# Token norms split in two steps, their squares summed on VectorE, in a hybrid decoder block

## The chip, the core and the metric

The kernel runs on one core of one Trainium2 chip. The metric is device time in microseconds of one execution of the whole program. Engines are named as the profile names them: PE is TensorE (matmuls), PEld its weight loads, DVE is VectorE, ACT is ScalarE, POOL is GpSimd, SP is SyncE, which issues most transfers. SBUF is the core's working memory of 128 partitions, PSUM the eight accumulator banks that TensorE writes.

## The reference

One decoder layer over 1024 tokens of 1024 channels, in float32: an RMS norm, one wide input projection that feeds a sparse attention and a pooling mixer, a gated merge with an output projection and a residual, then a second RMS norm, a squared-ReLU MLP with a residual, and a final RMS norm. What matters here are the last two norms and what stands around them:

```python
def rms_norm(x, g):
    xf = x.astype(jnp.float32)
    y = xf * lax.rsqrt(jnp.mean(xf * xf, axis=-1, keepdims=True) + EPS)
    return (y * g.astype(jnp.float32)).astype(x.dtype)
...
    x = x + (ga * a + gb * b) @ w_out
    h = rms_norm(x, norm_mlp)
    return x + jnp.square(jax.nn.relu(h @ w_ff1)) @ w_ff2
...
    return rms_norm(x, norm_final)
```

## The kernel before

The residual x lies transposed in SBUF: `acc` (printed as accx) holds eight blocks of 128 channels, each 1024 tokens wide, worked in two halves of 512 tokens. Because channels lie across partitions, the sum of squares of a token crosses partitions and is made by TensorE.

Every float32 matmul of 128x512 is done as three passes (L77 to L79, helper `mm3`): operands are split into a high part, cast by ACT (`whi`, `mv`, `mh`), and a low part, subtracted by VectorE (L82, `wlo`, `ml`). Weight tiles come through rings of a few buffers, so casts and subtractions work a few tiles ahead of TensorE.

A norm has these steps. Squares: `square_into` (L751) squares a finished block on ACT, the first into the sum `sqa`, each later one into `sq`, of which there is one buffer, and POOL adds it to `sqa` (L762); the last block's square stays apart. Sums: `sumsq_r` (L764) multiplies `sqa` and `sq` by a column of ones, one token block of 128 at a time, eight matmuls of one column (L769). Root: `rsqrt` (L117) is a chain of six small VectorE instructions (`rs_ms` to `rs_c`) with one square root on ACT between. Broadcast: `bcast` (L130) scales the identity by the four columns of roots into a tile that shares the buffer `sq` (L135), TensorE multiplies it by ones (L136), and ACT copies the result out of PSUM into `rB` (L137). Scaling: eight VectorE instructions multiply the blocks by gain and `rB`, into `h` (`normalise`, L785) or in place (`emit`, L880).

There are four such norms. The two ahead of the MLP are called norm 1 (first half of the tokens) and norm 2 (second half), the two final ones norm 3 and norm 4. Norm 1 stands between the second half's merge of branches (L798 to L812) and its output projection (L818 to L824). Norm 2 stands in the first MLP product, behind its step (1, 3) (L933). The MLP's two products are done by a scheme of seven half-size products with summed weights (PRODUCTS); in the second, each product p has eight steps j of 12 matmuls. Norm 3 is issued behind product 4 of the last round, whose results finish the first half, and norm 4 after product 3, the last (L971 to L973).

The framework orders the instructions of each engine from the order of the code and its own estimates; each engine runs its list in order and waits on semaphores.

Of the kernel before, what the change touches and what calls it, by code (L numbers as in the profile page):

```python
# [49 lines left out]
def build(tc, a, out, dbg=None):  # L50
# [697 lines left out]
    acc = accp.tile([P, NK, S], F32, name="accx")  # L748
    r2B = rB

    def square_into(sqs, src, m, sqa):  # L751
        n = src.shape[1]
        if m == 0:
            nc.scalar.activation(sqa[:, :n], src, AF.Square)
            sqs.append(sqa[:, :n])
        else:
            sq = accp.tile([P, HALF], F32, name="sq", bufs=1)[:, :n]
            nc.scalar.activation(sq, src, AF.Square)  # L758
            if m == NK - 1:
                sqs.append(sq)  # L760
            else:
                nc.gpsimd.tensor_tensor(sqa[:, :n], sqa[:, :n], sq, op=ADD)  # L762

    def sumsq_r(sqs, wk, ps_, dst):  # L764
        n = sqs[0].shape[1] // P
        ps = ps_()
        for j in range(n):
            for e, sq in enumerate(sqs):
                nc.tensor.matmul(ps[:, 2 * j:2 * j + 1], lhsT=sq[:, j * P:(j + 1) * P], rhs=ones[:, 0:1],  # L769
                                 start=e == 0, stop=e == len(sqs) - 1)  # L770
        col = wk.tile([P, NT], F32, name="rs_c", bufs=2)[:, :n]
        rsqrt(col, ps[:, 0:2 * n:2], wk, n)
        bcast(dst, col, ps_(), wk)

    psM = pool(root, "psM", bufs=8, space=PSUM)

    def bank():
        return psM.tile([P, HALF], F32, name="psm")
# [9 lines left out]
    with ExitStack() as st:  # L788
        wm = pool(st, "wm")
        for hf in range(2):  # L790
# [7 lines left out]
            for m in range(NK):  # L798
# [11 lines left out]
                nc.scalar.copy(mh, ta)  # L810
                sub(nc.vector, ml, ta, mh)
                mg.append((mh, ml))  # L812
            if hf == 1:
                sumsq_r(sqs, wm, bank, r2B[:, :HALF])
                normalise(0)
            sqa = accp.tile([P, HALF], F32, name="sqa", bufs=2)
            sqs = []
            for m in range(NK):  # L818
                wh, wl = load(cols(a["w_out"], m * P, P), nc.vector)
                nc.sync.dma_start(acc[:, m, sl], a["xT"][m * P:(m + 1) * P, sl])  # L820
                ps = bank()
                mm3(ps, [(wh[:, k], wl[:, k], mg[k][0], mg[k][1]) for k in range(NK)])
                nc.vector.scalar_tensor_tensor(acc[:, m, sl], ps, 0.5, acc[:, m, sl], op0=MUL, op1=ADD)
                square_into(sqs, acc[:, m, sl], m, sqa)  # L824
        dump("x2", acc)
    octx.close()

# [1 line left out]
    with ExitStack() as st:  # L829
# [43 lines left out]
            nc.scalar.activation(c, c, AF.Relu)  # L873
            nc.scalar.activation(c, c, AF.Square)

        def emit(n, sqs):
            sl = halves[n]
            sumsq_r(sqs, accp, bank, r2B[:, sl])
            for m in range(NK):
                nc.vector.scalar_tensor_tensor(acc[:, m, sl], acc[:, m, sl], gfin[:, m:m + 1], r2B[:, sl],  # L880
                                               op0=MUL, op1=MUL)
                if m % 2:
                    nc.sync.dma_start(out[(m - 1) * P:(m + 1) * P, sl].rearrange("(k p) t -> p k t", p=P),
                                      acc[:, m - 1:m + 1, sl])

        F = [wf.tile([P, S], F32, name=f"f{j}") for j in range(NF)]
        tt = nc.vector.tensor_tensor
        for fh in range(2):
# [4 lines left out]
            for pair in ((1, 2), (6,), (7, 4), (5, 3)):  # L893
# [9 lines left out]
                for p, j in steps:  # L903
# [26 lines left out]
                    elif p == 3:  # L930
                        tt(u, u, ps, op=ADD)
                        relu2(u)
                    if fh == 0 and (p, j) == (1, 3):  # L933
                        sumsq_r(sqs, accp, bank, r2B[:, HALF:])
                        normalise(1)


            if fh == 1:
                sqa_of = [accp.tile([P, HALF], F32, name="sqa", bufs=2) for _ in range(2)]
                fin = [[], []]  # L940
                nfin = [0, 0]

            def done(m, n):
                if fh == 1:
                    square_into(fin[n], acc[:, m, halves[n]], nfin[n], sqa_of[n])
                    nfin[n] += 1

            banks = {}
            group = {1: "x", 6: "x", 2: "y", 7: "z", 4: "z", 5: "w", 3: "w"}
            for p in (1, 2, 6, 7, 5, 4, 3):  # L950
                xt = PRODUCTS[p][1]
                fresh = group[p] not in banks
                if fresh:
                    banks[group[p]] = [bank() for _ in range(4)]
                ps = banks[group[p]]
                for j in range(JH):
                    xh, xl = moving([(blk_(k, n, j), sg_) for k, n, sg_ in xt])
                    wh, wl = weights("w_ff2", p, j)
                    for m in range(4):
                        mm3(ps[m], [(wh[:, m * P:(m + 1) * P], wl[:, m * P:(m + 1) * P], xh, xl)],  # L960
                            fresh and j == 0, j == JH - 1, not fresh)

                targets = {1: ((0, 0, 1),), 2: ((0, 0, 1),), 6: ((1, 1, -1), (1, 0, -1), (0, 1, 1)),
                           7: ((1, 1, 1),), 5: ((1, 1, -1),), 4: ((1, 0, 1),), 3: ((0, 1, 1),)}
                for m, n, sg_ in targets[p]:
                    for mi in range(4):
                        c = acc[:, m * 4 + mi, halves[n]]
                        tt(c, c, ps[mi], op=ADD if sg_ > 0 else SUB)
                        if p in (2, 5, 4, 3):
                            done(m * 4 + mi, n)  # L970
                if fh == 1 and p == 4:  # L971
                    emit(0, fin[0])
        emit(1, fin[1])  # L973
    root.close()


# [56 lines left out]
```

## Time and profile before

| | |
|---|---|
| median of 3 runs | 1509.44 us (1508.98 to 1510.2) |
| profiled execution, its own time | 1510.39 us |
| its span, first to last instruction | 1508.6 us |
| PE busy | 1451.2 us, 96% |
| DVE busy | 1001.3 us, 66% |
| ACT busy | 760.6 us, 50% |
| POOL busy | 187.6 us, 12% |
| mean granted clock of PE | 0.981 |

Busy shares are means over stages with different limits; a stage is read from the timeline around it. Matmul ends are modelled, so the pitch from start to start tells more than the durations. A float32 matmul of one column shows as two instructions. An engine's idle time is written behind the instruction that ended it, with what released it. The granted clock is a share of full speed: 1.00 is 2.4 GHz and 0.50 is 1.2 GHz.

### The profile page before, as it was taken

The page shows a single profiled execution, that of the slowest core. Times are in us where ns is not written, and L with a number is a line of the kernel's source. Part 1 is how long each engine was busy: PE and PEld are TensorE (multiplying, and loading weights), DVE is VectorE, ACT ScalarE, POOL GpSimd, SP SyncE. Part 2 cuts the span into 40 slices and gives each one's busy share as a digit, 9 for nine tenths or more (in the row PEclk, how much of TensorE's full clock was granted, in tenths as well). Part 3 has the DMA queues.
Part 4 walks back from the last instruction along what each step waited for, and adds up shares of the span by engine and source line. Part 5 has one row for each costly group of instructions (what it writes and reads, how often), then busy time and mean ns, then how long its engine had stood idle before and what let it go on. Part 6 is the DMA issues. An engine that isn't in the chain of part 4 may idle for free.

```text
span 1508.6 us, 20793 instructions
## 1 busy us (share of the span) xinstructions
PE 1451.2 (96%) x7369; PEld 1199.6 (80%) x7369; DVE 1001.3 (66%) x1928; ACT 760.6 (50%) x1561; POOL 187.6 (12%) x238
## 2 busy tenths in 40 slices
PE   8999999997999999999899999999999999999995
PEld 6788888886788878787687888888888888888874
DVE  5693451115888888777648368667897386679974
ACT  4454231115877877765334353674344545754441
POOL 2006323330111111110010100000000000001021
PEclk9999999998999999999999999999999999999997
DMA  8234217875668777867944333333332223332312
GB/s 304 70 99 148 70 49 192 213 191 147 179 162 201 177 184 178 196 157 188 323 136 147 113 91 98 96 93 97 98 98 92 97 86 103 98 98 84 109 53 112
DMA packets 130201, 204.67 MB, mean 136 GB/s; under 512 B 9904, under 2 KB 62896, under 8 KB 129584
## 3 DMA queue, kind: packets, MB, share of 16 engines
q1 hardware_dynamic: 112032, 136.22, 28.8%
q0 software_dynamic: 17920, 67.11, 19.5%
q8 instruction: 58, 0.95, 0.3%
q14 instruction: 47, 0.39, 0.1%
q10 hardware_dynamic: 144, 0.00, 0.0%
HBM read 186.52 MB, written 83.89 MB: 179 GB/s over the span
## 4 chain that ended last, share of the span: by engine, by line
PE 84%; DVE 6%; DMA 5%; ACT 3%; issue 1%; POOL 1%; SPq 0%; POOLq 0%; DVEq 0%; ACTq 0%
PE psm L78 16%; PE psm L77 16%; PE psm L79 16%; PE oacc L663 5%; PE psF L78 5%; PE psF L79 5%; PE psF L77 5%; PE psT L652 4%; PE psS L557 3%; PE psS L558 2%; PE psG L77 2%; PE psG L78 2%; PE psG L79 2%; DMA xt<-in_x 1%; PE psS L560 1%
## 5 line engine op out<-in xcount | busy, mean ns | idle before, releaser
L78 PE MATMUL psm<-mv,whi 128*128 128x512 f32 x896 | 351.5, 392 | 0.0
L79 PE MATMUL psm<-mv,wlo 128*128 128x512 f32 x896 | 351.3, 392 | 0.0
L77 PE MATMUL psm<-mv,whi 128*128 128x512 f32 x896 | 351.2, 392 | 0.0
L82 DVE TENSOR_TENSOR wlo<-wraw,whi 128x512 fp32r<-128x512 f32 x288 | 198.8, 694 | 98.8 <-ACT whi L866 70.2
L866 ACT CAST whi<-wraw 128x512 fp32r<-128x512 f32 x224 | 138.8, 620 | 247.8 <-PE psm L78 185.5
L78 PEld LDWEIGHTS psm<-mv,whi 128*128 128x128 f32 x896 | 168.7, 188 | 37.0
L77 PEld LDWEIGHTS psm<-mv,whi 128*128 128x128 f32 x896 | 168.7, 188 | 36.9
L79 PEld LDWEIGHTS psm<-mv,wlo 128*128 128x128 f32 x896 | 168.7, 188 | 36.6
L179 ACT CAST whi<-wraw 128x512 fp32r<-128x512 f32 x112 | 69.7, 622 | 124.5 <-PE psF L78 58.0
L762 POOL TENSOR_TENSOR sqa<-sqa,sq 128x512 f32<-128x512 f32 x24 | 33.4, 1392 | 734.3 <-ACT sq L758 734.3
L656 DVE TENSOR_TENSOR pl<-psT,ph 128x512 fp32r<-128x512 f32 (+1 forms) x160 | 102.0, 647 | 30.3 <-ACT ph L655 29.0
L655 ACT CAST ph<-psT 128x512 fp32r<-128x512 f32 (+1 forms) x160 | 87.8, 556 | 49.0 <-PE psT L652 47.2
L567 DVE TENSOR_REDUCE nm<-psS 128x1 f32<-128x64 f32 (+8 forms) x192 | 100.0, 540 | 17.2 <-PE psS L560 10.1
L82 POOL TENSOR_TENSOR wlo<-wraw,whi 128x512 fp32r<-128x512 f32 x48 | 65.6, 1368 | 108.1 <-ACT whi L179 88.2
L78 PE MATMUL psF<-xl,whi 128*128 128x512 f32 x192 | 74.7, 389 | 0.0
L77 PE MATMUL psF<-xh,whi 128*128 128x512 f32 x192 | 74.7, 389 | 0.0
L79 PE MATMUL psF<-xh,wlo 128*128 128x512 f32 x192 | 74.7, 389 | 0.0
L568 ACT ACTIVATE pS<-psS,nm 128x64 f32<-128x64 f32 (+8 forms) x128 | 68.0, 533 | 8.8 <-DVE nm L567 8.3
L846 ACT CAST mv<-mt 128x512 fp32r<-128x512 f32 x96 | 59.1, 617 | 20.0 <-DVE mt L844 15.5
L82 DVE TENSOR_TENSOR mv<-mt,mv 128x512 fp32r<-128x512 f32 x96 | 67.3, 708 | 1.1 <-ACT mv L846 0.6
L663 PE MATMUL oacc<-ph,vst 128*128 128x256 f32 x264 | 64.1, 318 | 1.2 <-ACT ph L655 0.9
L652 PE MATMUL psT<-cf,pS 128*128 128x128 f32 x352 | 60.4, 276 | 2.8 <-DVE pS L624 2.6
(242 smaller groups left out, 3034.7 us busy)
## 6 DMA issues: line engine op xcount, KB each, us to landing
wraw<-wsw_ff SPq DMA_DIRECT2D x128, 256.0 KB
wraw<-in_w_ff SPq DMA_DIRECT2D x96, 256.0 KB
wsw_ff<-in_w_ff POOLq DMA_DIRECT2D x16, 1024.0 KB, 9.4
wsw_ff<-wsw_ff POOLq DMA_DIRECT2D x16, 1024.0 KB, 9.3
wraw<-in_w_in SPq DMA_DIRECT2D x40, 256.0 KB
wraw<-in_w_out SPq DMA_DIRECT2D x32, 256.0 KB
xt<-in_x SPq DMA_DIRECT2D x8, 512.0 KB
qd<-q SPq DMA_DIRECT2D x16, 256.0 KB
```

The lines of the kernel that those rows point to most:

```text
L77: nc.tensor.matmul(ps, lhsT=sh, rhs=mh, start=first and i == 0, stop=False, skip_group_check=more)
L78: nc.tensor.matmul(ps, lhsT=sh, rhs=ml, start=False, stop=False, skip_group_check=more)
L79: nc.tensor.matmul(ps, lhsT=sl, rhs=mh, start=False, stop=last and i == n - 1, skip_group_check=more)
L82: eng.tensor_tensor(lo, src, f(hi), op=SUB)
L179: nc.scalar.copy(h, v)
L567: nc.vector.tensor_reduce(nm, v, axis=AX.X if flat else AX.XY, op=MAX, negate=True)
L568: nc.scalar.activation(p if flat else p.rearrange("p (a n) -> p a n", a=2), v, AF.Exp, bias=nm, accum_out=sm)
L652: nc.tensor.transpose(ps[:, j, e], src[e][:, c0:c0 + P], ident)
L655: nc.scalar.copy(ph[:, :n], ps[:, :n])
L656: nc.vector.tensor_tensor(pl[:, :n], ps[:, :n], f(ph[:, :n]), op=SUB)
L663: nc.tensor.matmul(o, lhsT=v, rhs=part[:rows, j], start=gi == 0 and j == 0 and part is ph, stop=2 * gi + j == nb - 1 and part is pl)
L866: nc.scalar.copy(hi, raw)
```

## The change

Four things change. The sums of squares are added on VectorE and not on POOL. `sumsq_r` is split: `stats` makes the sums and the root, and the broadcast is issued later, with matmuls of the running stage in between (norms 1 to 3). In the last product (p = 3) each of the four squares goes into a buffer of its own, taken from the ring of `mv`, and straight into the sums, so norm 4 has five tiles to sum and norm 3 one. `emit` multiplies by the broadcast where it lies in PSUM, without the copy into `rB`, and stores the last two blocks singly.

```diff
@@ -748,29 +748,28 @@
     acc = accp.tile([P, NK, S], F32, name="accx")
     r2B = rB
 
-    def square_into(sqs, src, m, sqa):
-        n = src.shape[1]
-        if m == 0:
-            nc.scalar.activation(sqa[:, :n], src, AF.Square)
-            sqs.append(sqa[:, :n])
+    def square_into(sqs, src, direct, sqa, sq=None):
+        if not sqs:
+            nc.scalar.activation(sqa, src, AF.Square)
+            sqs.append(sqa)
         else:
-            sq = accp.tile([P, HALF], F32, name="sq", bufs=1)[:, :n]
+            if sq is None:
+                sq = accp.tile([P, HALF], F32, name="sq", bufs=1)
             nc.scalar.activation(sq, src, AF.Square)
-            if m == NK - 1:
+            if direct:
                 sqs.append(sq)
             else:
-                nc.gpsimd.tensor_tensor(sqa[:, :n], sqa[:, :n], sq, op=ADD)
-
-    def sumsq_r(sqs, wk, ps_, dst):
-        n = sqs[0].shape[1] // P
-        ps = ps_()
-        for j in range(n):
-            for e, sq in enumerate(sqs):
+                nc.vector.tensor_tensor(sqa, sqa, sq, op=ADD)
+
+    def stats(sqs, wk):
+        ps = bank()
+        for e, sq in enumerate(sqs):
+            for j in range(4):
                 nc.tensor.matmul(ps[:, 2 * j:2 * j + 1], lhsT=sq[:, j * P:(j + 1) * P], rhs=ones[:, 0:1],
-                                 start=e == 0, stop=e == len(sqs) - 1)
-        col = wk.tile([P, NT], F32, name="rs_c", bufs=2)[:, :n]
-        rsqrt(col, ps[:, 0:2 * n:2], wk, n)
-        bcast(dst, col, ps_(), wk)
+                                 start=e == 0 and j == 0, stop=e == len(sqs) - 1 and j == 3)
+        col = wk.tile([P, NT], F32, name="rs_c", bufs=2)[:, :4]
+        rsqrt(col, ps[:, 0:8:2], wk, 4)
+        return col
 
     psM = pool(root, "psM", bufs=8, space=PSUM)
 
@@ -810,9 +809,7 @@
                 nc.scalar.copy(mh, ta)
                 sub(nc.vector, ml, ta, mh)
                 mg.append((mh, ml))
-            if hf == 1:
-                sumsq_r(sqs, wm, bank, r2B[:, :HALF])
-                normalise(0)
+            col = stats(sqs, wm) if hf == 1 else None
             sqa = accp.tile([P, HALF], F32, name="sqa", bufs=2)
             sqs = []
             for m in range(NK):
@@ -821,7 +818,10 @@
                 ps = bank()
                 mm3(ps, [(wh[:, k], wl[:, k], mg[k][0], mg[k][1]) for k in range(NK)])
                 nc.vector.scalar_tensor_tensor(acc[:, m, sl], ps, 0.5, acc[:, m, sl], op0=MUL, op1=ADD)
-                square_into(sqs, acc[:, m, sl], m, sqa)
+                square_into(sqs, acc[:, m, sl], m == NK - 1, sqa)
+                if hf == 1 and m == 0:
+                    bcast(r2B[:, :HALF], col, bank(), wm)
+                    normalise(0)
         dump("x2", acc)
     octx.close()
 
@@ -873,15 +873,20 @@
             nc.scalar.activation(c, c, AF.Relu)
             nc.scalar.activation(c, c, AF.Square)
 
-        def emit(n, sqs):
+        def emit(n, col):
             sl = halves[n]
-            sumsq_r(sqs, accp, bank, r2B[:, sl])
+            ps = bank()
+            dg = accp.tile([P, HALF], F32, name="sq", bufs=1)
+            for j in range(4):
+                js = slice(j * P, (j + 1) * P)
+                nc.vector.tensor_scalar(dg[:, js], ident, col[:, j:j + 1], None, op0=MUL)
+                nc.tensor.matmul(ps[:, js], lhsT=ones, rhs=dg[:, js], start=True, stop=True)
             for m in range(NK):
-                nc.vector.scalar_tensor_tensor(acc[:, m, sl], acc[:, m, sl], gfin[:, m:m + 1], r2B[:, sl],
-                                               op0=MUL, op1=MUL)
-                if m % 2:
-                    nc.sync.dma_start(out[(m - 1) * P:(m + 1) * P, sl].rearrange("(k p) t -> p k t", p=P),
-                                      acc[:, m - 1:m + 1, sl])
+                nc.vector.scalar_tensor_tensor(acc[:, m, sl], acc[:, m, sl], gfin[:, m:m + 1], ps, op0=MUL, op1=MUL)
+                step = 2 if m < NK - 2 else 1
+                if m % 2 or step == 1:
+                    nc.sync.dma_start(out[(m + 1 - step) * P:(m + 1) * P, sl].rearrange("(k p) t -> p k t", p=P),
+                                      acc[:, m + 1 - step:m + 1, sl])
 
         F = [wf.tile([P, S], F32, name=f"f{j}") for j in range(NF)]
         tt = nc.vector.tensor_tensor
@@ -930,20 +935,24 @@
                     elif p == 3:
                         tt(u, u, ps, op=ADD)
                         relu2(u)
-                    if fh == 0 and (p, j) == (1, 3):
-                        sumsq_r(sqs, accp, bank, r2B[:, HALF:])
+                    if fh == 0 and (p, j) == (1, 2):
+                        col = stats(sqs, accp)
+                    if fh == 0 and (p, j) == (1, 4):
+                        bcast(r2B[:, HALF:], col, bank(), accp)
                         normalise(1)
 
 
             if fh == 1:
                 sqa_of = [accp.tile([P, HALF], F32, name="sqa", bufs=2) for _ in range(2)]
                 fin = [[], []]
-                nfin = [0, 0]
 
             def done(m, n):
                 if fh == 1:
-                    square_into(fin[n], acc[:, m, halves[n]], nfin[n], sqa_of[n])
-                    nfin[n] += 1
+                    sq = None
+                    if p == 3:
+                        sq = xgp.tile([P, 2, HALF], F32, tag=f"xl{moving.n % MB}", name="sqd")[:, 0]
+                        moving.n += 1
+                    square_into(fin[n], acc[:, m, halves[n]], p == 3, sqa_of[n], sq)
 
             banks = {}
             group = {1: "x", 6: "x", 2: "y", 7: "z", 4: "z", 5: "w", 3: "w"}
@@ -959,6 +968,10 @@
                     for m in range(4):
                         mm3(ps[m], [(wh[:, m * P:(m + 1) * P], wl[:, m * P:(m + 1) * P], xh, xl)],
                             fresh and j == 0, j == JH - 1, not fresh)
+                    if fh == 1 and (p, j) == (3, 1):
+                        col = stats(fin[0], accp)
+                    if fh == 1 and (p, j) == (3, 2):
+                        emit(0, col)
 
                 targets = {1: ((0, 0, 1),), 2: ((0, 0, 1),), 6: ((1, 1, -1), (1, 0, -1), (0, 1, 1)),
                            7: ((1, 1, 1),), 5: ((1, 1, -1),), 4: ((1, 0, 1),), 3: ((0, 1, 1),)}
@@ -968,9 +981,7 @@
                         tt(c, c, ps[mi], op=ADD if sg_ > 0 else SUB)
                         if p in (2, 5, 4, 3):
                             done(m * 4 + mi, n)
-                if fh == 1 and p == 4:
-                    emit(0, fin[0])
-        emit(1, fin[1])
+        emit(1, stats(fin[1], accp))
     root.close()
 
 
```

VectorE at norm 1: before, the root (`rs_c`) is followed by the diagonal (`sq`) and all eight scalings into `h`, ahead of the next splits.

```order
L128 TENSOR_TENSOR rs_c<-rs_y,rs_t 128x4
L135 TENSOR_SCALAR sq<-cf,rs_c 128x128 x4
L785 SCALAR_TENSOR_TENSOR h_7964<-accx,cf,rB 128x512
L785 SCALAR_TENSOR_TENSOR h_7965<-accx,cf,rB 128x512
L785 SCALAR_TENSOR_TENSOR h_7966<-accx,cf,rB 128x512
L785 SCALAR_TENSOR_TENSOR h_7967<-accx,cf,rB 128x512
L785 SCALAR_TENSOR_TENSOR h_7968<-accx,cf,rB 128x512
L785 SCALAR_TENSOR_TENSOR h_7969<-accx,cf,rB 128x512
L785 SCALAR_TENSOR_TENSOR h_7970<-accx,cf,rB 128x512
L785 SCALAR_TENSOR_TENSOR h_7971<-accx,cf,rB 128x512
L82 TENSOR_TENSOR wlo<-wraw,whi 128x512
L823 SCALAR_TENSOR_TENSOR accx<-psm,accx 128x512
```

After, two splits of weight tiles and a residual add stand ahead of the scalings.

```order
L128 TENSOR_TENSOR rs_c<-rs_y,rs_t 128x4
L82 TENSOR_TENSOR wlo<-wraw,whi 128x512
L135 TENSOR_SCALAR sq<-cf,rs_c 128x128 x4
L820 SCALAR_TENSOR_TENSOR accx<-psm,accx 128x512
L82 TENSOR_TENSOR wlo<-wraw,whi 128x512
L784 SCALAR_TENSOR_TENSOR h_7964<-accx,cf,rB 128x512
L784 SCALAR_TENSOR_TENSOR h_7965<-accx,cf,rB 128x512
L784 SCALAR_TENSOR_TENSOR h_7966<-accx,cf,rB 128x512
```

The scalings (`h`) moved from ahead of the first residual add (`accx`) to behind it; six more of the eight follow the last row shown, then the second residual add and two splits.

PE at norm 3, in product 3 of the last round (`mv` are its moving operands, one tile for each step j): before, the first sum of ones and `sqa` stands behind one step, the rest in the next.

```order
L77 MATMUL psm<-mv_14325,whi 128x512
L78 MATMUL psm<-mv_14325,whi 128x512
L79 MATMUL psm<-mv_14325,wlo 128x512
L769 MATMUL psm<-ones,sqa 128x1
L77 MATMUL psm<-mv_14346,whi 128x512
L78 MATMUL psm<-mv_14346,whi 128x512
L79 MATMUL psm<-mv_14346,wlo 128x512
L77 MATMUL psm<-mv_14346,whi 128x512
L78 MATMUL psm<-mv_14346,whi 128x512
L769 MATMUL psm<-ones,sq 128x1
L769 MATMUL psm<-ones,sqa 128x1
```

After, four sums of `sqa` alone stand behind two steps and the first three matmuls of the third (`mv_14341`), and the broadcast behind that third step.

```order
L79 MATMUL psm<-mv_14341,wlo_14347 128x512
L768 MATMUL psm<-ones,sqa 128x1 x4
L77 MATMUL psm<-mv_14341,whi_14346 128x512
L78 MATMUL psm<-mv_14341,whi_14346 128x512
L79 MATMUL psm<-mv_14341,wlo_14347 128x512
L77 MATMUL psm<-mv_14341,whi_14346 128x512
L78 MATMUL psm<-mv_14341,whi_14346 128x512
L79 MATMUL psm<-mv_14341,wlo_14347 128x512
L77 MATMUL psm<-mv_14341,whi_14346 128x512
L78 MATMUL psm<-mv_14341,whi_14346 128x512
L79 MATMUL psm<-mv_14341,wlo_14347 128x512
L883 MATMUL psm<-sq,ones 128x128 x4
```

The sums moved from 12 matmuls behind product 4 to 27 behind it; between them and the broadcast (the line L883) stand nine matmuls.

VectorE at the same place after the change: the adds of squares stand between the residual adds, the splits of weights (`wlo`) and of moving operands (`mv`).

```order
L82 TENSOR_TENSOR mv_14427<-f_9185,mv_14427 128x512
L82 TENSOR_TENSOR wlo_14347<-wraw,whi_14346 128x512
L981 TENSOR_TENSOR accx<-accx,psm 128x512 x3
L762 TENSOR_TENSOR sqa<-sqa,sq 128x512
L981 TENSOR_TENSOR accx<-accx,psm 128x512
L82 TENSOR_TENSOR wlo<-wraw,whi 128x512
L762 TENSOR_TENSOR sqa<-sqa,sq 128x512
L82 TENSOR_TENSOR mv_14448<-f_9186,mv_14448 128x512
L82 TENSOR_TENSOR wlo<-wraw_14409,whi 128x512
L762 TENSOR_TENSOR sqa<-sqa,sq 128x512
L82 TENSOR_TENSOR mv_14469<-f_9187,mv_14469 128x512
L762 TENSOR_TENSOR sqa<-sqa,sq 128x512
```

Each add waits for its square on ACT; before, this list had the same splits without the adds.

## Rows read from the trace of the kernel before

**Rows 1.** Waits of PE, 760 to 1500 us: waiter, releaser, us in total, times, longest.

```profile
PE psm L769 <- POOL sqa L762: 7.6, 2, 4.8
PE psm L136 <- DVE sq L135: 5.0, 2, 3.1
```

**Rows 2.** Timeline of PE at norm 3: start, us, instruction, [idle before, releaser].

```profile
1454.73 0.39 PE L79 MATMUL psm<-mv,wlo 128*128 128x512 f32 x1
...
1457.45 0.39 PE L79 MATMUL psm<-mv,wlo 128*128 128x512 f32 x1
...
1460.61 0.38 PE L769 MATMUL psm<-ones,sqa 128*128 128x1 f32 x2 [2.77 <-POOL sqa L762]
...
1461.66 0.63 PE L77 MATMUL psm<-mv,whi 128*128 128x512 f32 x1
...
1469.50 0.48 PE L78 MATMUL psm<-mv,whi 128*128 128x512 f32 x1
```

**Rows 3.** Timeline of PE at norm 1.

```profile
806.56 0.39 PE L79 MATMUL psm<-oh,wlo 128*128 128x512 f32 x1
...
811.77 2.07 PE L136 MATMUL psm<-sq,ones 128*128 128x128 f32 x8 [3.14 <-DVE sq L135]
...
816.55 0.40 PE L78 MATMUL psm<-ml,whi 128*128 128x512 f32 x1
```

**Rows 4.** Timeline of PE at norm 2.

```profile
872.66 0.28 PE L769 MATMUL psm<-ones,sqa 128*128 128x1 f32 x2
...
874.36 0.49 PE L77 MATMUL psm<-mv,whi 128*128 128x512 f32 x1
...
876.78 1.05 PE L136 MATMUL psm<-sq,ones 128*128 128x128 f32 x8
...
877.59 0.47 PE L78 MATMUL psm<-mv,whi 128*128 128x512 f32 x1
```

**Rows 5.** Timeline of DVE at norm 1.

```profile
810.63 0.68 DVE L82 TENSOR_TENSOR ml<-ta,mh 128x512 fp32r<-128x512 f32 x1
```

**Rows 6.** Timeline of DVE and ACT at norm 4.

```profile
1494.68 0.16 DVE L122 TENSOR_SCALAR rs_ms<-psm 128x4 f32<-128x4 f32 x1 [7.93 <-PE psm L769]
...
1498.65 0.59 ACT L137 COPY rB<-psm 128x512 f32<-128x512 f32 x1 [3.57 <-PE psm L136]
...
1499.27 5.39 DVE L880 SCALAR_TENSOR_TENSOR accx<-accx,cf,rB 128x512 f32<-128x512 f32 x8 [2.20 <-ACT rB L137]
```

**Rows 7.** Timeline of DVE and ACT behind product 4.

```profile
1453.49 2.47 DVE L968 TENSOR_TENSOR accx<-accx,psm 128x512 f32<-128x512 f32 x4
...
1454.26 0.63 ACT L758 ACTIVATE sq<-accx 128x512 f32<-128x512 f32 x1 [0.89 <-DVE accx L968]
```

**Rows 8.** Groups of DVE by shape: line, operation, count, busy us, mean ns, idle.

```profile
L823 DVE SCALAR_TENSOR_TENSOR accx<-psm,accx 128x512 f32<-128x512 f32 x16 | 11.1, 691 | 23.4 <-PE psm L79 23.4
```

**Rows 9.** Timeline of PE at norm 4.

```profile
1485.63 0.39 PE L79 MATMUL psm<-mv,wlo 128*128 128x512 f32 x1
...
1490.83 0.59 PE L769 MATMUL psm<-ones,sqa 128*128 128x1 f32 x2 [4.81 <-POOL sqa L762]
...
1494.08 0.56 PE L769 MATMUL psm<-ones,sq 128*128 128x1 f32 x2
```

**Rows 10.** Stretches: length, busy of PE, PEld, DVE, ACT, POOL, clock, DMA share, GB/s.

```profile
809.00:810.00 1.00, 0.00 (x0) 0.00 (x0) 1.00 (x3) 0.60 (x2) 0.00 (x0) 0.82 0.00 0
...
1409.00:1433.00 24.00, 24.00 (x107) 19.69 (x106) 23.96 (x41) 9.76 (x16) 0.00 (x0) 1.00 0.29 94
...
1488.00:1489.00 1.00, 0.00 (x0) 0.00 (x0) 0.00 (x0) 0.19 (x1) 0.78 (x1) 0.94 0.00 0
...
1506.00:1507.00 1.00, 0.00 (x0) 0.00 (x0) 0.00 (x0) 0.00 (x0) 0.00 (x0) 0.50 1.00 389
```

**Rows 11.** Timeline of POOL and DVE behind product 5.

```profile
1438.79 1.56 POOL L762 TENSOR_TENSOR sqa<-sqa,sq 128x512 f32<-128x512 f32 x1 [0.74 <-ACT sq L758]
...
1439.12 1.78 DVE L844 TENSOR_TENSOR mt<-mt,f 128x512 f32<-128x512 f32 x1
```

## The prediction

> **What bounds the kernel now.** I read three views, in this order. First the list of waits of TensorE (PE) over the second half of the span: there are only two entries, 7.6 us for the POOL sums of squares and 5.0 us for the diagonal that carries a norm back to all partitions [rows 1]. So from there on the kernel is a stream of matmuls that stops only at the token norms. Second, the timeline around each of the four norms; the pitch of the stream is read between two matmuls that stand twelve apart, 1454.73 and 1457.45, so 2.72 / 12 = 0.227 us [rows 2]. Third, the stretches with their granted clock: 1.00 is the level of 2.4 GHz, 0.50 that of 1.2 GHz. A norm costs what lies between the matmul ahead of it and the first one at full clock behind it, less 0.227 for each matmul between.
>
> **Norm 1 (first half, ahead of the output projection).** From 806.56 to 816.55 are 9.99 us [rows 3], with 8 pitches (1.82) of real work (in the program's order seven projection matmuls stand between the broadcast and 816.55): 8.17 us for the norm. In it lie 3.14 us of waiting for the diagonal, and those seven matmuls at half clock. The change keeps the sums where they are, and puts the broadcast behind the 24 matmuls of the first output block. Norm 2 shows what the two parts cost at full clock with work between: sums 874.36 - 872.66 = 1.70, broadcast 877.59 - 876.78 = 0.81 [rows 4]. So 8.17 - 2.51 = 5.66 us go.
>
> What the stall hid comes out now. The low part of the last merged block ends at 811.31 [rows 5]; TensorE needs it 1.70 + 22 x 0.227 us behind 806.79, at 813.48, so 2.2 us are left. Next, VectorE: the eight scalings into h (5.39 us, as the same form x8 in [rows 6]) now stand behind the broadcast and one ACT square (0.63 [rows 7]) and copy (0.59 [rows 6]) in the middle of the projection. The broadcast ends at 806.79 + 1.70 + 5.45 + 0.81 = 814.75, the scalings run 816.0 to 821.4, then come the residual add and the split of a weight tile, 0.69 each [rows 8], to 822.8. TensorE wants that tile's low part at 814.75 + 5.45 + 2.72 + 0.45 = 823.4. So 0.6 us of cover; I take off 0.2 for semaphores. Gain **5.4**; bounds 2.0 (a wait of 2 us for the split, and the clock falls for seven matmuls again) and 5.7.
>
> **Norm 2.** Sums and broadcast run between matmuls already, at 1.70 + 0.81 and clock 1; both only move, the scalings some 3 us later. The pair of products behind it still lasts eight weight tiles, so I count nothing; bounds -0.5 and +1.
>
> **Norm 3 (first half, final).** From 1457.45 to 1469.50 are 12.05 us [rows 2] with 14 pitches (3.18): 8.87 us. 2.77 are the wait for POOL, whose sums stand in a chain of square, add, square on one buffer; the rest is that the clock falls at 1461.66, where matmuls stretch to 0.63. After: the sum is one tile, so four column matmuls for eight (0.85), and 0.81 for the broadcast, with nine matmuls between. The adds are on VectorE. Its first residual add starts at 1453.49, the first square at 1454.26 [rows 7]; then each of the four links is a square 0.63, an add of 0.69, and one or two splits queued ahead of the add. Following VectorE's order row by row I get the last add at 1461.05. TensorE arrives behind 27 matmuls of the last product: 1454.96 + 27 x 0.227 = 1461.09. So it is level; I allow 0.2 us there. The reciprocal chain and the diagonal need about 2.3 us from the sums (1494.68 to 1498.65, less the 2.07 that the broadcast takes at half clock [rows 3, 6], and one diagonal block), TensorE's nine matmuls give 2.04: 0.3 us more. Gain 8.87 - 0.85 - 0.81 - 0.5 = **6.7**; bounds 3.5 (3 us of wait, and the clock falls) and 7.2.
>
> **Norm 4 (the end).** The last matmul starts at 1485.63 and frees TensorE at 1485.86. Before, the four last squares alternate with three POOL adds, and the sums begin only at 1490.83 with the clock already down; rs_ms follows at 1494.68 and the scalings at 1499.27 [rows 6, 9]. After, the four last squares go to TensorE as they are, in buffers of their own: ACT needs 0.63 each, TensorE 20 column matmuls. At 1.70 / 8 = 0.2125 that is 4.25 us, and ACT is done long before, so TensorE sets the end. Then 0.17 to rs_ms as before (the last sum starts at 1494.08 and gives way 0.43 later, rs_ms at 1494.68 [rows 6, 9]), and from rs_ms to the scalings 4.59 less the copy out of PSUM (1498.65 to 1499.27, 0.62 gone) = 3.97. The scalings would start at 1485.86 + 4.25 + 0.17 + 3.97 = 1494.25, 5.0 earlier, if the clock stays up.
>
> It probably doesn't: in this tail it falls within 1488 to 1489 (0.94 over that stretch, so at 1488.88 [rows 10]), 3.0 us after TensorE came free, and at norm 1 within 809 to 810 (0.82 [rows 10]; at 809.64), 2.85 us after the sums began and 1.2 after they ended; so the narrow sums do not hold it up. At norm 3 it fell 3.7 us after the stream stopped. At half clock a column matmul takes twice as long, 0.43. With the fall 2.9 to 3.7 us in, 3 to 7 of the 20 are slow: 0.6 to 1.4 us lost. I take 1.2 and a gain of **3.8**; all 20 slow would leave 0.7, none 5.0.
>
> The scalings read PSUM now. One such instruction with a PSUM operand takes 691 ns [rows 8], one of the eight with all of it in SBUF 5.39 / 8 = 0.67 in a row: no cost. The Trainium skill, page "VectorE: DVE Perf Modes", section "Rules for kernel authors", advises to copy PSUM to SBUF first where many operations will read it; by that the copy's 0.62 us would be worth keeping and this gain 3.2. The row does not bear it out for this fp32 form with two tensor operands.
>
> The finer last transfers (one block each instead of two) bring nothing: with the output leaving, the DMA engines run at share 1.00 and 389 GB/s until 1507 [rows 10], so the end is set by when the first pair leaves.
>
> **VectorE's added load.** 22 adds of 0.69 = 15.2 us, 12 of them in the projection, 10 in the last stage. POOL's 24 go, and with them collisions: a two-input VectorE instruction takes 1.78 us instead of 0.69 while a POOL add runs [rows 11]. So each of the ten gives back up to 1.1 for its 0.69; net zero. It matters because VectorE is busy 23.96 of 24.00 us ahead of the sum [rows 10], yet TensorE waits for no split there [rows 1].
>
> **Sum.** 5.4 + 6.7 + 3.8 = 15.9 us. From the profiled execution's 1510.39 that gives 1494.5; the median of the runs shown lies 0.95 lower, from there 1493.5. Forecast **1494.0**; its own range is 1491 to 1497.
>
> **Rivals.**
> 1. Norm 3 stays a stall: VectorE's in-order queue holds an add behind splits, and the square that waits for the single buffer holds ACT's casts in turn. For it: estimate and need meet within 0.1 us. Against: only one split per link. Price: 3 us of wait, a further fall of the clock of 2 to 3 us: 1499.
> 2. The final sums run wholly at half clock, or the scalings block a split at norm 1: 3 us back each: 1497.
> 3. Slower: all VectorE adds land on TensorE's path, 22 x (0.69 + 0.63 of waiting for the square in the same queue) = 29 us against 15.9 gained: 1523.5. It decides once VectorE is later than the four weight tiles it works ahead, 4 x 2.72 = 10.9 us. The full VectorE stretch [rows 10] speaks for it, the absence of any wait for splits, with POOL's collisions costing about as much today [rows 11], against.
> 4. Stalls gone but the clock or the order differs per execution so that little is left: within 3 us of before (0.2%, about the least that a measurement of this kernel tells from no change).
>
> Chances: forecast 70%, rival 1 12%, rival 2 12%, rival 3 3%, rival 4 3%. The range 1491 to 1499 reaches to rivals 1 and 2. Faster 0.94, within 0.2% 0.03, slower 0.03.
>
> **What would show it.** In the profile after: no wait for POOL; between the last branch matmul and the first output matmul about 1.7 us with the clock at 1.00 throughout; at norm 3 four column matmuls, a gap under 0.5 us, clock 1.00; in the tail 20 column matmuls starting within 0.3 us of the last wide one, some of them at 0.43, the scalings starting about 8.4 to 10 us behind it, and about 9.3 us from there to the end as now. It is wrong if TensorE waits over 1 us for a split (L82) or a square, or if the clock falls at norms 1 or 3.

## The result, and the profile after

The changed kernel takes 1494.47 us (median of 6 runs, 1488.6 to 1499.15) where the kernel before takes 1510.05 (6 runs, 1508.98 to 1511.78): a ratio of 0.9891, 95% interval 0.9872 to 0.9909, or 15.6 us less. Forecast were 1494.0. Executions of the changed kernel spread over some 10 us, so the account below goes by stages of the trace. The profiled execution took 1493.06 us, its span 1491.3, mean clock 0.989.

Two profiled spans lie 17.3 us apart, and the starts of TensorE's matmuls tell where. The last branch matmul ahead of norm 1 starts 0.57 us earlier (the code ahead of it is the same but for the engine of some adds; more on that in the last section). Each later stage is measured from one matmul to another, so that this drops out. A wide matmul is one of 128x512, a column matmul one with a single column of ones.

| stage | before, us | changed, us | gain | forecast |
|---|---|---|---|---|
| norm 1 | 8.17 | 2.72 | 5.45 | 5.4 |
| norm 2 | 2.51 | the same | 0 | 0 |
| norm 3 | 8.87 | 1.79 | 7.08 | 6.7 |
| last wide matmul to the end (norm 4) | 22.97 | 18.77 | 4.2 | 3.8 |

The gain at norm 3 is a difference of starts: the last matmul of product 4 starts 6.02 us earlier than before, the last wide matmul of the kernel 13.10, so 7.08 us lie between; the 1.79 is what that leaves of 8.87.

TensorE at norm 1 in the changed kernel (timeline: start, us, instruction, idle before it and releaser; `x8` are eight records, two to a matmul in these rows):

```profile
805.99 0.39 PE L79 MATMUL psm<-oh,wlo 128*128 128x512 f32 x1
806.22 0.95 PE L768 MATMUL psm<-ones,sqa 128*128 128x1 f32 x8
807.03 1.03 PE L768 MATMUL psm<-ones,sq 128*128 128x1 f32 x8
...
813.52 1.05 PE L136 MATMUL psm<-sq,ones 128*128 128x128 f32 x8
814.33 0.48 PE L77 MATMUL psm<-mh,whi 128*128 128x512 f32 x1
814.64 0.40 PE L78 MATMUL psm<-ml,whi 128*128 128x512 f32 x1
```

No row carries an idle time, and nothing runs at half clock, where [rows 3] have 3.14 us of waiting and a broadcast of 2.07. From 805.99 to 814.64 are 8.65 us with 26 pitches of 0.228 (5.93): 2.72 for the norm.

TensorE at norm 3, and the last add of squares on VectorE:

```profile
1454.29 0.69 DVE L762 TENSOR_TENSOR sqa<-sqa,sq 128x512 f32<-128x512 f32 x1
...
1454.85 0.40 PE L79 MATMUL psm<-mv,wlo 128*128 128x512 f32 x1
1455.08 1.00 PE L768 MATMUL psm<-ones,sqa 128*128 128x1 f32 x8
...
1458.13 1.05 PE L883 MATMUL psm<-sq,ones 128*128 128x128 f32 x8
1458.94 0.47 PE L77 MATMUL psm<-mv,whi 128*128 128x512 f32 x1
1459.25 0.39 PE L78 MATMUL psm<-mv,whi 128*128 128x512 f32 x1
```

The add ends at 1454.98, TensorE starts the sums at 1455.08: level, as worked out, and not late here. Read by itself, the norm costs 1459.25 - 1454.85 = 4.40 us less 11 pitches of 0.227, 1.9 us. Set against [rows 2], the wait of 2.77 us for POOL and the matmuls of 0.63 are gone.

The tail: PE and VectorE, the broadcast of before in a row of its own, and one stretch of the changed kernel with the clock (length, busy of PE, PEld, DVE, ACT, POOL, clock, DMA share, GB/s).

```profile
1472.53 0.39 PE L79 MATMUL psm<-mv,wlo 128*128 128x512 f32 x1
1472.76 0.95 PE L768 MATMUL psm<-ones,sqa 128*128 128x1 f32 x8
1473.57 4.09 PE L768 MATMUL psm<-ones,sqd 128*128 128x1 f32 x32
...
1477.69 0.16 DVE L122 TENSOR_SCALAR rs_ms<-psm 128x4 f32<-128x4 f32 x1 [4.05 <-PE psm L768]
...
1479.47 2.08 PE L883 MATMUL psm<-sq,ones 128*128 128x128 f32 x8 [1.82 <-DVE sq L882]
...
1481.59 5.36 DVE L885 SCALAR_TENSOR_TENSOR accx<-accx,cf,psm 128x512 f32<-128x512 f32 x8 [1.58 <-PE psm L883]
```

```profile
1496.54 2.07 PE L136 MATMUL psm<-sq,ones 128*128 128x128 f32 x8 [1.90 <-DVE sq L135]
```

```profile
1476.00:1477.00 1.00, 1.00 (x10) 1.00 (x9) 0.00 (x0) 0.00 (x0) 0.00 (x0) 0.87 0.00 0
```

The sums start without the 4.81 us of [rows 9]; the mean clock of 0.87 puts the fall to half clock at 1476.74, 4.0 us behind the last product, and the broadcast takes 2.08 us at half clock where it took 2.07. Of PE's waits from 760 us on, one is left: the diagonal in the tail, 1.8 us.

```profile
PE psm L883 <- DVE sq L882: 1.8, 1, 1.8
```

### The profile page after: what moved, and what is told of

Same layout as the page of the kernel before. It is cut to its first block, busy times and chain, and to the rows that moved or that the text cites. A ratio compares the mean times of both kernels' runs of the same rounds, so it can differ in the third digit from the quotient of the medians.

```text
span 1491.3 us, 20797 instructions
## 1 busy us (share of the span) xinstructions
PE 1443.1 (97%) x7385; PEld 1193.7 (80%) x7385; DVE 1006.1 (67%) x1950; ACT 759.2 (51%) x1559; POOL 154.1 (10%) x214
## 4 chain that ended last, share of the span: by engine, by line
PE 87%; DVE 5%; DMA 3%; ACT 2%; issue 1%; POOL 0%; SPq 0%; DVEq 0%; ACTq 0%; POOLq 0%
PE psm L79 16%; PE psm L77 16%; PE psm L78 16%; PE oacc L663 6%; PE psF L78 5%; PE psF L79 5%; PE psF L77 5%; PE psT L652 4%; PE psS L557 3%; PE psS L558 2%; PE psG L77 2%; PE psG L78 2%; PE psG L79 2%; DMA gb<-gbd 1%; PE psS L560 1%
## 5 line engine op out<-in xcount | busy, mean ns | idle before, releaser
L77 PE MATMUL psF<-bhi,xh 128*128 128x256 f32 (+1 forms) x192 | 55.6, 293 | 5.7 <-DVE vst L270 4.4
```

The lines of the kernel that those rows point to most:

```text
L77: nc.tensor.matmul(ps, lhsT=sh, rhs=mh, start=first and i == 0, stop=False, skip_group_check=more)
```

## The experiments

The time is a median, its ratio is to the kernel before run beside it, with the 95% interval. Each kernel was profiled once. Where a few us or less matter, I read stages of the trace: the last branch matmul to the last wide one ("middle": 679.07 us before, 666.54 changed) and the last wide one's start to the end ("tail": 22.97 and 18.77). The planner is the part of the framework that orders each engine's instructions.

**e1: one part alone, the adds.** In the kernel before:

```diff
-                nc.gpsimd.tensor_tensor(sqa[:, :n], sqa[:, :n], sq, op=ADD)
+                nc.vector.tensor_tensor(sqa[:, :n], sqa[:, :n], sq, op=ADD)
```

> The kernel before with one edit, the adds of squares on VectorE; sums, broadcasts and the tail are its own. Theory (at norm 3 the stall is the late POOL sum against a planner that puts the first column sum 12 matmuls behind product 4; with the adds on VectorE the order of TensorE's instructions changes by itself, the first column sum 21 matmuls behind and the rest 24): three adds end 6.1 us behind the first residual add, TensorE arrives 6.0 us behind it, so norm 3 costs 8 columns (1.7) + broadcast 0.81 + at most 0.6 of wait = 2.5 to 3.1 us instead of 8.87, without a fall of the clock. Norm 1 stays at 8.17 us. In the tail three links of square and add go from 2.0 us to about 1.4 each: 1.8 us earlier. Together 7.6 to 8.2 us under the kernel before, about 1502. Rival (norm 3 is cured by splitting its code in two): norm 3 stays at 7 to 9 us, only the tail moves, 1.8 us, about 1508.

Measured: 1503.32 us (ratio 0.9933, 0.9913 to 0.9954); middle 672.31, tail 20.67. Norm 3:

```profile
1458.60 0.39 PE L79 MATMUL psm<-mv,wlo 128*128 128x512 f32 x1
1458.82 0.31 PE L769 MATMUL psm<-ones,sqa 128*128 128x1 f32 x2
...
1459.79 0.28 PE L769 MATMUL psm<-ones,sq 128*128 128x1 f32 x2
...
1461.27 0.48 PE L77 MATMUL psm<-mv,whi 128*128 128x512 f32 x1
...
1463.69 1.05 PE L136 MATMUL psm<-sq,ones 128*128 128x128 f32 x8
```

No wait, no half clock; the first column matmul stands 21 matmuls behind product 4 and the rest 24, as expected. The middle is 6.76 us shorter, 0.57 of that at norm 1, where the clock came back earlier: norm 3 is 6.2 us cheaper by this one line. The theory holds; the rival, that splitting the code cures norm 3, is out. The tail gives 2.3 instead of 1.8.

**e2: the complement.** The changed kernel with `nc.gpsimd` in that line.

> The changed kernel with its adds of squares back on POOL. Theory: the sums at norm 3 now stand 24 matmuls behind product 4 (TensorE there 6.9 us behind the first residual add); four POOL links of about 2.0 us end 9.1 us behind it, so TensorE waits about 2.2 us, and 1 to 2 us more if the clock falls; norms 1, 2 and 4 don't change, since their POOL adds end long before. 2 to 4 us over the changed kernel. Rival A (the engine of the adds does not matter, only the moved steps do): within 0.5 us of the changed kernel at norm 3. Rival B (collisions of POOL and VectorE reach TensorE): waits for splits in the last stage, more than 5 us over.

Measured: 1495.91 us (ratio 0.9893, 0.987 to 0.9916); middle 668.86, 2.3 over the changed kernel's.

```profile
1457.24 1.05 PE L768 MATMUL psm<-ones,sqa 128*128 128x1 f32 x8 [2.10 <-POOL sqa L762]
```

The wait has the forecast size, the clock stays up, and there is no wait for a split: ten VectorE instructions take 1.2 to 1.8 us beside a POOL add, as in [rows 11], and cost TensorE nothing here. Both rivals are out. With everything else changed, the engine of the adds is worth 2.3 us in the middle, 2.1 of them this wait; the whole times, with ratios of 0.9893 and 0.9891, do not tell the two kernels apart. The sums stand 24 matmuls behind product 4 here and 27 in the changed kernel.

**e3: norm 1 in one piece.** The changed kernel with this ahead of the projection, and without its broadcast behind block 0:

```diff
-            col = stats(sqs, wm) if hf == 1 else None
+            if hf == 1:
+                bcast(r2B[:, :HALF], stats(sqs, wm), bank(), wm)
+                normalise(0)
```

> The changed kernel with the broadcast and the scalings of norm 1 put back directly behind its sums. Theory: the stall comes back whole: from the last branch matmul to the 26th projection matmul 14.1 us instead of 8.65, with about 3.1 us of waiting for the diagonal and half clock for some matmuls; span 5.4 us longer. Rival (norm 1 became cheap because VectorE's and POOL's work around it changed): less than 1 us longer.

Measured: 1503.44 us (ratio 0.9933, 0.9911 to 0.9954); middle 672.13, 5.6 longer.

```profile
812.77 0.39 PE L79 MATMUL psm<-oh,wlo 128*128 128x512 f32 x1
...
817.98 2.07 PE L136 MATMUL psm<-sq,ones 128*128 128x128 f32 x8 [3.13 <-DVE sq L135]
819.70 0.77 PE L77 MATMUL psm<-mh,whi 128*128 128x512 f32 x1
...
821.39 0.40 PE L78 MATMUL psm<-ml,whi 128*128 128x512 f32 x1
```

The stall is back, with 4.8 us rather than 5.4, since the clock returned three matmuls earlier than in [rows 3]. The other 0.8 us is a pitch of 0.233 us instead of 0.229 over the next 16 times 12 matmuls, at clock 1.00; its cause stays open.

**e4: the code of norm 3 in one piece.**

```diff
-                    if fh == 1 and (p, j) == (3, 1):
-                        col = stats(fin[0], accp)
-                    if fh == 1 and (p, j) == (3, 2):
-                        emit(0, col)
...
+                if fh == 1 and p == 4:
+                    emit(0, stats(fin[0], accp))
```

> The changed kernel with the code of norm 3 put back in one piece behind product 4. Theory: the planner places the four column sums 27 matmuls behind product 4 and the broadcast nine further on, whichever way the code is written, so norm 3 stays at about 1.8 us and the time is that of the changed kernel; its runs also show how far that kernel's executions scatter (1488.6 to 1499.2 so far). Rival (the split in the code is what cures norm 3): the sums wait again, 3 to 7 us longer.

Measured: 1496.81 us (1491.03 to 1500.23, 6 runs; ratio 0.9889, 0.9869 to 0.991); middle 666.53, the changed kernel's to 0.01. On every engine the instructions run in the changed kernel's order. So at norm 3 splitting the code did nothing. The adds' engine alone moves the sums (e1), and so does the rest of the change without it (e2: from 12 to 24 matmuls); that it is the single tile in that rest was not tested.

**e5: the copy kept.** In `emit`, `nc.scalar.copy(r2B[:, sl], ps)` and the scalings read `r2B`.

> The changed kernel with the broadcast copied out of PSUM by ACT ahead of the final scalings, as before. Read in the tail alone (from the last wide matmul to the end; the stages ahead of norm 1 scatter by more than this). Theory: the copy is 0.6 us on the chain from the broadcast to the first scaling and the eight scalings take 5.4 us either way (5.36 us from PSUM, 5.39 from SBUF), so the tail is 0.6 us longer, 19.0 to 19.3 us against 18.3 to 18.7. Rival (the Trainium skill, page "VectorE: DVE Perf Modes", section "Rules for kernel authors": copy to SBUF first where many operations read PSUM): the scalings run faster from SBUF and the first store leaves as early as now; the tail stays within 0.2 us.

Measured: 1494.43 us (one run), tail 18.96.

```profile
1480.20 2.08 PE L883 MATMUL psm<-sq,ones 128*128 128x128 f32 x8 [1.82 <-DVE sq L882]
...
1482.94 5.39 DVE L887 SCALAR_TENSOR_TENSOR accx<-accx,cf,rB 128x512 f32<-128x512 f32 x8 [2.20 <-ACT rB L884]
```

From broadcast to scaling are 2.74 us where the changed kernel has 2.12, so the copy costs 0.62 us on the path, and eight scalings take 5.39 from SBUF, 5.36 from PSUM. The tail as a whole is only about 0.2 longer, at the edge of what the rival allows: the clock fell 0.8 us later than in the changed kernel, and the column matmuls took 4.5 us, not 4.9. So the stage decides here, not the tail. The Trainium skill, page "VectorE: DVE Perf Modes", section "Rules for kernel authors", has two ways for work on a matmul's output: to accept the plain speed from PSUM, or to copy to SBUF first where many operations follow. For this instruction the copy gains nothing.

**e6 and e7: the stores.** `step = 2` throughout (four pairs), and `step = 1 if m < 2 else 2` (first two single).

> The changed kernel with its final stores in four pairs of blocks, as before. From the first final scaling to the end the kernel before takes 9.32 us and the changed one 9.67. Theory A (my prediction: the transfers are bound by bandwidth, single stores bring nothing and cost nothing): 9.67 stays within 0.1. Theory B (the extra last store costs its own issue and completion): 9.3 us.

> The changed kernel with the first two blocks stored singly, the other six in pairs. The stream of stores starts 2.35 us behind the first scaling, runs 5.5 us at about 385 GB/s, and one block is scaled in 0.67 us, one block stored in 0.69. Theory (the end is set by when the first store leaves): the stream starts one scaling, 0.67 us, earlier and so does the end; from the first scaling to the end 8.7 to 9.0 us. Rival (each store costs a fixed time at its issue or the scalings cannot keep up): 9.3 us or more.

Measured: e6 1493.86 us, 9.3 us from first scaling to end; e7 1498.5 us, 9.6 (one run each; their spans differ ahead of norm 1). Theory B holds in e6: with five stores the end lies 0.35 us later behind the first scaling than with four, and all profiles of five (9.6 to 9.7 us) and of four (9.3) agree. The last data leave at about the same distance; what differs lies behind them. The changed kernel (end at 1491.3), then e6 (end at 1492.1):

```profile
1489.40:1489.50 0.10, 0.00 (x0) 0.00 (x0) 0.00 (x0) 0.00 (x0) 0.00 (x0) 0.50 0.47 164
1489.50:1489.60 0.10, 0.00 (x0) 0.00 (x0) 0.00 (x0) 0.00 (x0) 0.00 (x0) 0.50 0.03 0
```

```profile
1490.60:1490.70 0.10, 0.00 (x0) 0.00 (x0) 0.00 (x0) 0.00 (x0) 0.00 (x0) 0.50 0.40 144
1490.70:1491.00 0.30, 0.00 (x0) 0.00 (x0) 0.00 (x0) 0.00 (x0) 0.00 (x0) 0.50 0.01 0
```

From the last data to the end are 1.7 us with five stores and 1.3 with four. In e7 the rival holds: the stream starts 0.7 us earlier, runs dry, and gains nothing:

```profile
1489.50:1490.00 0.50, 0.00 (x0) 0.00 (x0) 0.50 (x2) 0.00 (x0) 0.00 (x0) 0.50 1.02 393
1490.00:1490.50 0.50, 0.00 (x0) 0.00 (x0) 0.50 (x2) 0.00 (x0) 0.00 (x0) 0.50 0.24 90
```

**e8: fewer columns.** The last two steps of product 3 go bank by bank (`held` keeps their operands), and the first two of the four squares are added on VectorE:

```diff
+                    if (fh, p, j) == (1, 3, JH - 2):
+                        continue
...
-                        mm3(ps[m], [(wh[:, m * P:(m + 1) * P], wl[:, m * P:(m + 1) * P], xh, xl)],
+                        mm3(ps[m], [(h_[:, ms_], l_[:, ms_], a_, b_) for h_, l_, a_, b_ in held],
...
-                    square_into(fin[n], acc[:, m, halves[n]], p == 3, sqa_of[n], sq)
+                    square_into(fin[n], acc[:, m, halves[n]], p == 3 and m % 4 > 1, sqa_of[n], sq)
```

> The changed kernel with the last two steps of product 3 ordered by block (six matmuls for each of the four banks in turn), the squares of the first two of these blocks added on VectorE and only the last two summed directly: 12 column matmuls instead of 20. Theory (in the tail TensorE's 20 column matmuls set the end, 4.9 us): the last square ends about 1.8 us behind the last wide matmul and its four columns 0.85 later, so the scalings start 6.3 to 6.6 us behind the end of the last wide matmul instead of 8.8, tail 16.0 to 16.5 us instead of 18.3 to 18.7. Rival (the last square, not the columns, is late): no more than 1 us earlier.

Measured: 1491.23 us (ratio 0.9866, 0.9826 to 0.9907); tail 16.87.

```profile
1470.31 1.05 PE L768 MATMUL psm<-ones,sqa 128*128 128x1 f32 x8
1471.22 1.93 PE L768 MATMUL psm<-ones,sqd 128*128 128x1 f32 x16
...
1474.96 2.07 PE L883 MATMUL psm<-sq,ones 128*128 128x128 f32 x8 [1.82 <-DVE sq L882]
```

The columns set the end: 12 take 2.84 us, 20 took 4.90. The gain is 1.9 us and the tail of 16.87 lies above the 16.0 to 16.5 expected, since the columns end 1.4 us behind the last square and not 0.85. They run without a gap, so the last square is not what is late, and the rival's 1 us is exceeded.

**e9 and e11: keeping the clock.** e8 with four stores, and two (e9, shown) or one (e11) matmuls whose result nobody reads:

```diff
-        emit(1, stats(fin[1], accp))
+        col = stats(fin[1], accp)
+        warm = bank()
+        for _ in range(2):
+            nc.tensor.matmul(warm, lhsT=ones, rhs=fin[1][-1], start=True, stop=True)
+        emit(1, col)
```

> The kernel of e8 with the four paired stores again (worth 0.35 us by e6) and, between the last column sum and the broadcast, two extra matmuls of 128x512 whose result nobody reads (0.82 us each at full clock) in the 1.8 us in which TensorE waits for the diagonal. In e8 the clock falls 3.7 us behind the last product, 0.8 us behind the last column sum, and the broadcast then takes 2.08 us where norms 1 to 3 show 0.81 at full clock. Theory A (wide work ahead keeps the clock up): broadcast to first scaling 0.85 instead of 2.1, tail 16.83 - 0.35 - 1.25 = 15.2 us. Theory B (the clock falls at the same moment whatever is put behind the columns): the extra matmuls run partly at half clock and hold up the broadcast, tail 16.5 to 17.3 us.

> The kernel of e9 with one extra matmul instead of two. In e9 the two end 3.2 us behind the last column sum's start and the broadcast starts 0.43 us behind the first diagonal block. Theory: one extra matmul is enough to keep the clock up until the broadcast, which then starts 0.3 us behind the first diagonal block's start; scalings start 5.7 to 6.2 us behind the end of the last product, tail 15.2 to 15.6 us; against the changed kernel on the same chip 3 us (0.2%) less in the median, which the scatter ahead of norm 1 may hide. Rival: one is too little, the clock falls ahead of the broadcast as in e8 (2.08 us), tail 16.5 us.

Measured: e9 1494.07 us (ratio 0.9862, 0.9832 to 0.9891), tail 15.6; e11 1492.74 us (ratio 0.9863, 0.9845 to 0.988), tail 16.5. First e9, with the clock in a stretch of its broadcast, then e11, with the clock behind its extra matmul:

```profile
1481.15 1.96 PE L995 MATMUL psm<-sqd,ones 128*128 128x512 f32 x4
1483.20 1.13 PE L883 MATMUL psm<-sq,ones 128*128 128x128 f32 x8
```

```profile
1483.00:1484.00 1.00, 0.92 (x8) 0.83 (x8) 0.64 (x4) 0.00 (x0) 0.00 (x0) 1.00 0.00 0
```

```profile
1478.76 1.16 PE L995 MATMUL psm<-sqd,ones 128*128 128x512 f32 x2
1480.81 2.05 PE L883 MATMUL psm<-sq,ones 128*128 128x128 f32 x8 [0.89 <-DVE sq L882]
```

```profile
1479.00:1480.00 1.00, 0.92 (x2) 0.03 (x1) 0.62 (x5) 0.21 (x1) 0.00 (x0) 0.84 0.00 0
```

With two, the clock stayed up in the profiled execution until 1486.55, behind all of TensorE's work, and the broadcast took 1.13 us where e8's took 2.07. The tail of 15.6 is above Theory A's 15.2: 0.35 of the gain over e8 come from the four paired stores and 0.9, not 1.25, from the clock. With one matmul the clock fell at 1479.67, and the tail of 16.5 is e8's less the store; the rival holds. One profile each: that two always keep the clock and one never does was not shown, and the whole times, with ratios of 0.986 for e8, e9 and e11 alike, do not tell them apart.

**e10: three stores.** e8 with stores of two, two and four blocks.

> The kernel of e8 with three final stores, of two, two and four blocks, instead of five. From the first final scaling to the end: five stores 9.67 and 9.61 us, four 9.32. Theory A (each store adds about 0.35 us to the end, at its completion): 8.97. Theory B (only the size or the lateness of the last store counts): the last store of four blocks starts later and larger, 9.3 us or more.

Measured: 1495.16 us (one run), 10.7 us from first scaling to end. Theory B holds: the store of four waits for its last scaling, and the queue stands empty meanwhile.

```profile
1487.00:1488.00 1.00, 0.00 (x0) 0.00 (x0) 1.00 (x2) 0.00 (x0) 0.00 (x0) 0.50 0.79 303
1488.00:1489.00 1.00, 0.00 (x0) 0.00 (x0) 0.07 (x1) 0.00 (x0) 0.00 (x0) 0.50 0.00 0
```

From the last data to the end are 1.5 us here, more than with four stores, so a fixed price for each store is not shown; why a fifth costs 0.35 us stays open.

**e12: the changed kernel again, beside e11.**

> The changed kernel as it is, on the same chip as e11, to set their medians side by side. Theory (the scatter of single executions comes from ahead of norm 1, where the programs are the same): from the last branch matmul to the last wide matmul 666.5 us and tail 18.3 to 18.8 us again, while the last branch matmul starts anywhere from 803 to 813 us. Rival (the changed norms themselves differ from execution to execution): the 666.5 us move by more than 1 us, with half clock at norm 1 or 3.

Measured: 1496.88 us (ratio 0.9884, 0.9867 to 0.99); on the same chip e11 is 4.1 us lower in the median, 2.9 of it in the tails of the two profiles. Middle 666.50, as expected; the tail 19.4, longer than the 18.3 to 18.8 expected: the clock fell at 1479.54, 3.2 us behind the last product, so more columns were slow.

```profile
1479.00:1480.00 1.00, 1.00 (x9) 1.00 (x8) 0.00 (x0) 0.00 (x0) 0.00 (x0) 0.77 0.00 0
```

## Why the prediction was right

The stages bear it out one by one. That the median lies 0.5 us from the forecast is partly luck: executions of the changed kernel spread from 1488.6 to 1499.15 us, and the 15.6 us between the medians is less than the 16.7 that the stages of the two profiles give.

- **Norm 1.** 5.45 us against 5.4. The order held and no split is waited for, so the 0.6 us of cover was enough; e3 brings the stall back.
- **Norm 2.** Nothing, as forecast: the shift of TensorE's stream is 6.02 us both behind norm 1 and at the end of product 4.
- **Norm 3.** 7.08 against 6.7. The last add and TensorE met within 0.1 us, and the 0.5 us allowed for waits was hardly needed. The trace of before showed the POOL wait; it could not show that moving the adds alone moves the sums (e1), and that the split in the code does nothing (e4). By the measure that the prediction uses in the tail, the clock fell 3.9 us behind the stream at norm 3 before, not 3.7; nothing hangs on it.
- **Norm 4.** 4.2 against 3.8, from three errors that partly cancel. The clock's fall cost 0.65 us (4.90 for the columns, less 4.25), not 1.2; the chain from sums to scalings was 0.2 shorter; the stores in single blocks, costed at nothing, took 0.35.
- **VectorE's added load.** Net zero for TensorE holds, but the collisions I set against it were no cost either: e2 has them back, and the middle is longer by 2.3 us, of which 2.1 are its wait for POOL.
- **The step that failed** is "the finer last transfers bring nothing", with the end "set by when the first pair leaves". They cost 0.35 us: from the first scaling to the end are 9.67 us, not 9.3 as before. The data take as long as before, 5.7 us; what lies behind them was not looked at: 1.7 us with five stores, 1.3 with four (e6). And in e7 the first store leaves earlier and the end does not.
- **The rivals.** Neither a stall at norm 3, nor all sums at half clock, nor exposed adds appeared, nor was little left. e12 shows the second in part: its clock fell 0.8 us earlier, its columns took 5.6 us for 4.9, and 0.6 of the gain went.

Where the 16.7 us from norm 1 on come from: the split at norm 1 4.8 to 5.5, the adds' engine 6.2 at norm 3 and 2.3 in the tail (e1). What is left was not measured part by part: 0.9 at norm 3, where the single tile is the likely cause, and 1.9 in the tail, for direct sums and the missing copy less the fifth store. These parts overlap: taken from the finished kernel, the adds' engine is worth 2.3 (e2), since the sums then stand late anyway.

## What to carry to other kernels

When a planner orders the instructions, look at the order before writing a split: one operand's engine can move a matmul further than moved code. A reduction's broadcast belongs behind as many matmuls as its small chain lasts, and in a tail the count of narrow matmuls is itself the path. Compare small changes from matmul to matmul within a trace; whole times scatter by more than a change of one or two us.

## What the hardware showed beyond that

The scatter of 10 us between executions lies ahead of norm 1. The last branch matmul starts at 803.34 us in e8 and 812.77 in e3, with the same code ahead of it; behind it, the middles of the changed kernel agree to 0.04 us. Of these 9.4 us, 3.3 come in one stretch: the mean clock from 340 to 380 us was 0.96 in e8 (first row) and 0.83 in e3. Over half of the rest lies in earlier stretches of the same kind: from 50 to 70 us and from 130 to 150 us e3 had 0.91 and e8 1.00. Why the clock differs between executions stays open.

```profile
340.00:380.00 40.00, 32.39 (x198) 25.64 (x199) 26.31 (x98) 26.45 (x103) 4.27 (x6) 0.96 0.57 156
```

```profile
340.00:380.00 40.00, 31.76 (x173) 26.03 (x172) 21.30 (x80) 19.79 (x77) 5.20 (x5) 0.83 0.53 131
```

In the tails of all the changed kernels but e9, and of e1, the clock fell 3.2 to 5.3 us behind the last wide matmul, at no fixed distance, so one kernel's tail moved by 0.6 us (18.77 and 19.40).
